# Later attention loads, borrowed buffers for two Fourier evictions, and a rearranged start in a hybrid encoder layer

## The chip, the cores and the metric

The kernel runs on one core of a Trainium2 chip. The core has a matrix engine (TensorE, PE in the profile; its weight loads run beside it as PEld), a vector engine (DVE), a scalar engine (ACT), GpSimd (POOL), and a sync engine (SP) that here only issues DMAs. Each engine works through its own queue in order; they wait for each other by semaphores. The metric is the device time of one execution in microseconds (us), as the median of several runs.

## The reference

One layer of an encoder is applied to two batches of 2048 rows of 1024 features, with the same weights. Rows are normalised, projected into six blocks of columns (q, k, v, the attention gate ga, the Fourier input f and its gate gf), and go through two branches:

```
u = rmsnorm(h, g_norm)
q, k, v, ga, f, gf = split(u @ w_in)
q, k = rope(rmsnorm(q, g_q)), rope(rmsnorm(k, g_k))
a  = attention(q, k, v) * silu(ga)                   # 8 q heads, 2 kv heads, width 64
fo = real(fft2(f over rows, channels)) @ w_fmix * silu(gf)
h  = h + concat(a, fo) @ w_out
h  = h + (p @ w_ple) * sigmoid(rmsnorm(h, g_ple) @ w_ple_gate)
y  = rmsnorm(h, g_final)
```

All is in float32. The kernel makes float32 products on TensorE from float16 pairs (a high part and a residual, three products each).

## The kernel before

There are two parts. **project()** runs over 16 chunks of two tiles of 128 rows (eight chunks for each batch). For a chunk it loads the rows x, squares them on ACT (sq_u), takes a reciprocal root on DVE (newton), writes the high part on ACT (hi_u) and the residual on DVE, and has SP transpose both by DMA into uc (lo_u). PE multiplies uc with the weights of kv and q (mm_tile), and in a sweep with those of f, gf and ga (sweep_f, sweep_ga). ACT evicts, DVE and POOL do norms and rope, and SP stores q, k and v transposed to DRAM (qTd, kTd, vd); POOL's queue stores gates and the first Fourier stage (gd). The second part interleaves **attention()** (64 units of eight steps; a unit is a batch, a kv head and 128 queries) with the second Fourier stage (**fourier2()**), then with the output projection.

The order of everything in project() is written out by hand: within an engine the instructions stand as the code calls them. What the change touches:

- **The weights** (weights(), line 293). A block of w_in comes in eight pieces of 128 rows. For each block DVE scans all eight for the largest magnitude (L312), POOL reduces that over partitions, DVE makes a scale from it (L272 to L328), and then for each piece ACT writes the high part (L334) and DVE the residual (L335). Only then can PE use it. It is a generator: a `next` takes one step (a load, a scan, a split), and `until(g, "loaded")` or `until(g, "split")` runs it to that point. There are generators for kv, q, ga, and one in rest() for f, gf and what is wanted later.
- **The places of the pieces** (places()). In the early phase, pieces are loaded into buffers of the pool A1 that other tiles will use later: names such as qn, t2, z, t1. f's and gf's pieces take a ring of ten 2-KB buffers (w2k, shown as w_st).
- **The written-out start** (lines 839 to 900), before the loop `for i in range(2, n + 4): iteration(i)`. It interleaves the first chunks (0 to 4 of the 16) with the weights. The maxima of v (VL, the vmax instructions) release the kv products' banks in PSUM.
- **early()** (L1682), called at iteration n - 3. It closes the pool of x and the high/residual tiles and opens the pool kv in its place; attention() up to its first `yield` then issues on SP the loads of k and v of both kv heads and of q for units 0, 1 and 2; fourier_first() opens the pool F0 and loads the tables and rows for the first two Fourier tiles (c2, c2x, g_in).
- **leads()** runs the row maxima (a_mx, L1193) of attention's first units inside project()'s last iterations. They use PSUM banks of the pool ps_x that the sweeps use too.
- **fourier2()** evicts the first products of each tile t into fT (L1079), a tile of the pool B, which takes memory that project()'s tiles had. mix() then multiplies fT with bd, which SP loads first of all in fourier2().
- **The exponentials' buffers** are seven tiles p32 of the pool att, each [128, 2, 512] in float32 (L1149).

SP's queue is where loads, transposes and stores of project() stand in one line. A store of v (vd) frees the tile vs, which ACT writes again two chunks later (L679).

Of the kernel before, what the change touches and what calls it, by code (L numbers as in the profile page):

```python
# [10 lines left out]
F32 = mybir.dt.float32  # L11
# [25 lines left out]
FP = 2  # L37
# [3 lines left out]
P32 = 7  # L41
# [99 lines left out]
class Build:  # L141
# [421 lines left out]
        v = self.a["x_prompt" if s == 0 else "x_sample"]  # L563
        return v.rearrange("o (t r) d -> t (o r) d", t=NT)[t]

    def project(self, P, PU, W, early, wkv, wq, wga, bg, mid):

# [215 lines left out]
        def iteration(i):  # L785
            nonlocal stores, stores_next
            if ok(i + 4):
                load_x(i + 4, 0)
            if ok(i - 1):
                load_rope(i - 1)  # L790
            stores, stores_next = stores_next, []
            for f in stores:
                f()
            del stores[:]
            if ok(i + 3):
                sq_u(i + 3)
            sq = square_z(i - 1) if ok(i - 1) else None
            if ok(i - 1) and i > 2:
                VL.pop((i - 1, 1))()
            if ok(i - 3):  # L800
                lo_q(i - 3)
            if ok(i - 2):
                rope_q(i - 2)
            rs = None
            if ok(i - 1) or ok(i + 2):
                rs = newton(i - 1 if ok(i - 1) else None, i + 2 if ok(i + 2) else None, sq)
            if ok(i):
                mm_tile(i, 0)
            if ok(i):
                sweep_part(4.0)  # L810
                VL.pop((i, 0))()
            sweep_part(1000.0 if i < n else (6.0, 9.0, 5.0, 100.0)[i - n])
            if ok(i - 1):
                norm_q(i - 1, rs)
            if ok(i + 2):
                hi_u(i + 2)
                for tt in range(CH):
                    lo_u(i + 2, tt)
            if ok(i + 4):
                load_x(i + 4, 1)  # L820
            if ok(i - 2):
                hi_q(i - 2)
            if ok(i):
                mm_tile(i, 1)
                append(i)
            if i == n - 3:
                early()
            if i == n + 3:
                self.drain(bg)
                self.drain(self.ahead)  # L830
                self.last_stores = nc.gpsimd
                for f in stores_next:
                    f()
                del stores_next[:]

        both = lambda f, i: [f(i, tt) for tt in range(CH)]
        both(load_x, 0)
        until(wkv, "loaded")  # L840
        both(load_x, 1)
        sq_u(0)
        newton(None, 0, None)
        hi_u(0)
        for _ in range(3):
            next(wkv)
        both(lo_u, 0)
        until(wq, "loaded")
        until(wkv, "split")
        both(mm_kv, 0)  # L850
        until(bg, "loaded")
        sq_u(1)
        for _ in range(4):
            next(wq)
        newton(None, 1, None)
        hi_u(1)
        for _ in range(5):
            next(wq)
        lo_u(1, 0)
        next(wq)  # L860
        lo_u(1, 1)
        until(wq, "split")
        both(mm_q, 0)
        both(load_x, 2)
        load_rope(0)
        for _ in range(4):
            next(wga)
        both(mm_tile, 0)
        VL.pop((0, 0))()
        both(mm_kv, 1)  # L870
        both(mm_q, 1)
        until(bg, "split")
        until(wga, "loaded")
        load_x(3, 0)
        both(mm_tile, 1)
        for x in ((0, 1), (1, 0), (1, 1)):
            VL.pop(x)()
        for f in stores_next:
            f()
        del stores_next[:]  # L880
        append(0)
        until(bg, "split")
        sweep_part(10.4)
        sq_u(2)
        newton(None, 2, None)
        hi_u(2)
        both(lo_u, 2)
        load_x(3, 1)
        both(load_x, 4)
        until(bg, "split")  # L890
        next(bg)
        sweep_part(11.6)
        mid()
        sq_u(3)
        make_u(3, 0)
        both(load_x, 5)
        sq_u(4)
        sweep_part(1000.0)
        append(1)
# [83 lines left out]
    def fourier2(self, pool, hook):  # L983
# [82 lines left out]
        for t in range(16):  # L1066
# [2 lines left out]
                yield "half"  # L1069
            loads(t + FP)  # L1070
            g, c = [G.pop((t, i)) for i in range(2)], C.pop(t)
            fT = pool.tile([128, 4, 2, 128], F32, name="fT", bufs=2)
            fx = None
            for i in range(2):
                ps = self.bank()
# [40 lines left out]
    def attention(self, kvp):  # L1116
# [136 lines left out]
        for kv in range(2):  # L1253
            load_kv(0, kv)
            load_q(kv)
        load_q(2)
        nm = kvp.tile([128, 4, 128], F16, name="nm", bufs=1)
        nc.gpsimd.memset(nm[:], 0.0)
        kone = kvp.tile([128, 128], F16, name="kone", bufs=1)
# [15 lines left out]
                    max_rows(0)  # L1275

        self.ahead = leads()
        pool = yield 0.0
        self.ones = pool.tile([128, 64], F32, name="ones", bufs=1)
        nc.gpsimd.memset(self.ones[:], 1.0)  # L1280
        fresh = {last[0, kv]: kv for kv in range(2)}
# [389 lines left out]
    def run(self):  # L1671
# [5 lines left out]
        with pool("psA", 5, space=PSUM) as self.psX, pool("A", side="right") as A:  # L1677
            with pool("A1", side="right") as A1:
# [3 lines left out]
                def early():  # L1682
                    u_stack.close()
                    KV = w_stack.enter_context(pool("kv"))
                    self.atts = self.attention(KV)
                    next(self.atts)
                    self.fourier_first(w_stack.enter_context(pool("F0")))

                W, self.WF = {}, {}
# [7 lines left out]
                WP = w_stack.enter_context(pool("wts", 3))  # L1697
                held = {}

                def places(tags, m):  # L1700

                    def stage(k, cols):
                        if k % m == 0:
                            tag, n = tags[k // m]
                            held[tag, k // m] = A1.tile([128, m, cols], F32, name="w_" + tag, tag=tag, bufs=n)
                        t = held[tags[k // m][0], k // m]
                        if k % m == m - 1:
                            del held[tags[k // m][0], k // m]
                        return t[:, k % m, :]
                    return stage  # L1710

                def stage(k, cols):
# [5 lines left out]
                        return self.WF[n]  # L1718
                    return go

                wkv = self.weights([block("kv", lambda: W["kv"])], places([("qn", 1), ("t2", 1)], 4), 8)
                wq = self.weights([block("q", lambda: W["q"])], places([("z", 2), ("z", 2), ("t1", 2), ("t1", 2)], 2), 8)

                def mid():
                    self.setup2(A1)
                    self.scales()
                    self.scale_a()

                wga = self.weights([block("ga", wtile("ga"))], places([("qn", 1), ("t2", 1), ("t1", 2), ("t1", 2)], 2), 8)

                def rest():
                    wf = self.weights([block(n, wtile(n)) for n in ("f", "gf")], stage, 8)
                    for g, scale in ((wf, self.scale_f), (wf, self.scale_gf), (wga, self.scale_ga)):
                        for x in g:
                            if x == "split":
                                scale()
                            yield x
                            if x == "split":
                                break
                    yield True  # L1740
                    for n in range(2):
                        c = slice(n * 512, (n + 1) * 512)
                        yield from self.weight_far(f"wo{n}", a["w_out"][0][:, c], 512, None, A1)
# [3 lines left out]
                    yield from self.channel_map(A1)  # L1747
                    self.scales3()

                self.project(A1, AU, W, early, wkv, wq, wga, rest(), mid)  # L1750
                manual.__exit__(None, None, None)
        self.psX = None
        att_stack = ExitStack()
        WP1 = w_stack.enter_context(pool("wts1"))
        AP = att_stack.enter_context(pool("att"))
        self.psS = att_stack.enter_context(pool("psS", 2, space=PSUM))
        self.psM = att_stack.enter_context(pool("psM", 1, space=PSUM))
        self.psO = att_stack.enter_context(pool("psO", 1, space=PSUM))
# [104 lines left out]
```

## Time and profile before

| | |
|---|---|
| median of 3 runs | 2685.51 us (2683.37 to 2689.4) |
| profiled execution | 2686.84 us, span 2685.1 us |
| PE busy | 2615.4 us, 97% |
| DVE, ACT, POOL busy | 1612.6, 1186.0, 1634.4 us |
| mean granted PE clock | 0.992 |
| moved by DMA | 305.37 MB, mean 114 GB/s |

The profile is of one execution. Rows of the timeline give start, duration, engine, line and operation, output and inputs, and in brackets the idle time just before with what ended it; SPq is SP issuing a DMA (no busy time). Rows of stages give the busy time of PE, PEld, DVE, ACT and POOL with counts in brackets, then the clock granted to PE, the share of DMA engines busy and GB/s. Rows of waits give who waited for whom, in total, how often, and the longest. Rows of DMA issues give the size of one and the median time from issue to landing.

### The profile page before, as it was taken

The page shows a single profiled execution, that of the slowest core. Times are in us where ns is not written, and L with a number is a line of the kernel's source. Part 1 is how long each engine was busy: PE and PEld are TensorE (multiplying, and loading weights), DVE is VectorE, ACT ScalarE, POOL GpSimd, SP SyncE. Part 2 cuts the span into 40 slices and gives each one's busy share as a digit, 9 for nine tenths or more (in the row PEclk, how much of TensorE's full clock was granted, in tenths as well). Part 3 has the DMA queues.
Part 4 walks back from the last instruction along what each step waited for, and adds up shares of the span by engine and source line. Part 5 has one row for each costly group of instructions (what it writes and reads, how often), then busy time and mean ns, then how long its engine had stood idle before and what let it go on. Part 6 is the DMA issues. An engine that isn't in the chain of part 4 may idle for free. (4 is left out here: it accounts for less than half of the span.)

```text
span 2685.1 us, 49976 instructions
## 1 busy us (share of the span) xinstructions
PE 2615.4 (97%) x20096; PEld 1401.6 (52%) x20096; DVE 1612.6 (60%) x2300; ACT 1186.0 (44%) x1983; POOL 1634.4 (61%) x1376
## 2 busy tenths in 40 slices
PE   5899999999999999999999999999999999999998
PEld 3465565655556664545455554444454544555443
DVE  6756565565446675666675656655565666656634
ACT  4543333333224553554444545445444444444442
POOL 1233232242236886787787777777777877777760
PEclk9999999999999999999999999999999999999999
DMA  8467576685617774222322223332232322232222
GB/s 238 133 178 200 175 195 188 165 196 145 172 56 207 238 214 111 55 62 74 80 68 66 60 68 91 97 74 67 69 87 62 74 77 76 63 83 75 64 76 73
DMA packets 453385, 305.37 MB, mean 114 GB/s; under 512 B 294272, under 2 KB 394816, under 8 KB 453152
## 3 DMA queue, kind: packets, MB, share of 16 engines
q1 hardware_dynamic: 440240, 260.41, 37.9%
q0 software_dynamic: 12912, 41.77, 4.2%
q8 instruction: 157, 2.57, 0.4%
q14 instruction: 76, 0.62, 0.1%
HBM read 149.50 MB, written 86.51 MB: 88 GB/s over the span
## 5 line engine op out<-in xcount | busy, mean ns | idle before, releaser
L1166 POOL TENSOR_TENSOR acc<-acc,p 128x1024 f32<-128x1024 f32 x384 | 919.9, 2396 | 195.7 <-ACT p L1161 159.6
L1193 DVE TENSOR_REDUCE a_mx<-ps_m 128x1 f32<-128x1024 f32 x498 | 609.3, 1223 | 564.1 <-PE ps_m L1185 555.2
L1161 ACT ACTIVATE p<-ps_s,s_scale 128x512 f32<-128x512 f32 x1024 | 648.1, 684 | 653.6 <-PE ps_s L1158 647.0
L1472 PE MATMUL ps_g<-w_pg,hT 64*128 64x512 f16 x2784 | 493.1, 376 | 1.5 <-DVE h L1398 0.8
L451 PEld LDWEIGHTS <-uc 128*128 128x128 f16 x3072 | 301.9, 98 | 320.8 <-issue 33.0
L1221 PE MATMUL ps_o<-p,v 128*64 128x256 f32 x4096 | 467.7, 381 | 0.0
L1158 PE MATMUL ps_s<-q,k 64*128 64x512 f16 x3072 | 433.7, 378 | 5.1 <-ACT p L1161 4.9
L1221 PEld LDWEIGHTS ps_o<-p,v 128*64 128x64 f32 x4096 | 288.6, 137 | 166.0 <-issue 27.7
L1472 PEld LDWEIGHTS <-hT 64*128 64x128 f16 x2784 | 205.2, 94 | 155.7 <-issue 13.5
L1472 PE MATMUL ps_g<-w_wo,mh 64*128 64x512 f16 x1440 | 259.8, 377 | 1.2 <-DVE seen L1438 1.2
L1472 PE MATMUL ps_g<-w_wo,mT 64*128 64x512 f16 x1440 | 256.2, 376 | 0.0
L1158 PEld LDWEIGHTS <-k 64*128 64x128 f16 x3072 | 151.1, 94 | 200.0 <-issue 76.9
L1185 PE MATMUL ps_m<-k,q 64*128 64x512 f16 x996 | 200.0, 377 | 4.5 <-DVE a_mx L1193 4.3
L1164 POOL TENSOR_TENSOR acc<-p,p 128x1024 f32<-128x1024 f32 x64 | 150.9, 2358 | 69.3 <-ACT p L1161 68.7
L451 PEld LDWEIGHTS <-w_ga 128*128 128x128 f16 x1536 | 149.2, 98 | 39.3 <-issue 11.1
L935 POOL DMA_DIRECT2D gfd<-gt x32 | 19.7, 616 | 234.3 <-DVE gt L963 201.0
L1472 PEld LDWEIGHTS <-mh 64*128 64x128 f16 x1440 | 100.1, 94 | 90.8 <-issue 18.0
L1472 PEld LDWEIGHTS <-mT 64*128 64x128 f16 x1440 | 102.7, 94 | 81.3 <-issue 3.8
L1243 DVE RECIPROCAL ps_f<-ps_f 128x256 f32<-128x256 f32 x63 | 110.7, 1756 | 21.2 <-PE ps_f L1236 21.2
L451 PE MATMUL ps_x<-w_f,uc 128*128 128x512 f16 x480 | 105.9, 379 | 0.0
L451 PE MATMUL ps_x<-uc,w_ga 128*128 128x256 f16 x936 | 105.5, 273 | 0.0
L1228 ACT ACTIVATE at<-ps_o,a_scale 128x256 f32<-128x256 f32 x64 | 30.3, 474 | 165.9 <-PE ps_o L1221 165.9
(319 smaller groups left out, 3188.5 us busy)
## 6 DMA issues: line engine op xcount, KB each, us to landing
q<-qTd SPq DMA_DIRECT2D x256, 64.0 KB, 2.3
ag<-agd SPq DMA_DIRECT2D x64, 256.0 KB, 3.3
out<-h POOLq DMA_DIRECT2D x31, 512.0 KB, 3.0
x<-in_x_prompt SPq DMA_DIRECT2D x16, 512.0 KB, 5.0
gfd<-gt POOLq DMA_DIRECT2D x32, 256.0 KB, 2.7
gd<-ge POOLq DMA_DIRECT2D x32, 256.0 KB, 2.9
agd<-gat POOLq DMA_DIRECT2D x64, 128.0 KB, 3.0
w_st<-in_w_out SPq DMA_DIRECT2D x32, 256.0 KB, 3.8
```

What stands on the lines that cost most here:

```text
L451: self.nc.tensor.matmul(ps, lhs(ia, k), rhs(ib, k), start=(i == 0), stop=(i == 3 * ks - 1))
L935: lambda t=t, gt=gt: nc.gpsimd.dma_start(self.gfd[s][t], gt[:]))
L1158: nc.tensor.matmul(S[u][e][:], w[sl], q[sl].rearrange("p h q -> p (h q)"), start=j == i == 0, stop=i + 1 == len(todo), skip_group_check=True)
L1161: nc.scalar.activation(p[:, e, :], S[u][e][:], AF.Exp, scale=self.sc["s_scale"][:])
L1164: nc.gpsimd.tensor_tensor(out=ACC[u][:], in0=P[u, 0][:], in1=p[:], op=ALU.add)
L1166: nc.gpsimd.tensor_tensor(out=ACC[u][:], in0=ACC[u][:], in1=p[:], op=ALU.add)
L1185: nc.tensor.matmul(ps[c], Q[u][0][sl, h, :], kt[s, kv, half][sl, :, 0, :], start=True, stop=True)
L1193: nc.vector.reduce_max(MX[u][:, h, half, c:c + 1], x, axis=AX.X)
L1221: nc.tensor.matmul(o[64 * f:64 * f + 64], vt[s, kv, c // 8][:, c % 8, :], p[:, e, f], start=(c == 0), stop=(c == 15))
L1228: nc.scalar.activation(at[:].rearrange("p c q -> p (c q)"), o, AF.Copy, scale=self.sc["a_scale"][:])
L1243: nc.vector.reciprocal(r, r)
L1472: nc.tensor.matmul(g[0][:], g[1](ia, k)[sl], g[2](ib, k)[sl], start=a, stop=z, skip_group_check=True)
```

## The change

It has three parts.

**Late loads.** early() still loads k and v of both heads and q of units 0 and 1. A new function later(), called at iteration n, three iterations on, loads q of unit 2 and runs fourier_first().

**Fourier evictions.** fT of the first two Fourier tiles is taken from the exponentials' buffers, p32 of the pool att, instead of the pool B.

**The start.** q's first five pieces are loaded ahead of the first transposes, the rest right behind them, and x of chunk 1 after that. q's scans come before the reciprocal root of chunk 1, and q's whole split before chunk 1's high parts and residuals. f, gf and ga have a generator each; gf's pieces go into buffers of uc, qs and qT. ga's and gf's pieces are loaded together after f's split; x of chunk 3 and half of chunk 4 are loaded right behind those pieces, and chunk 2 is normalised before gf's split instead of after it. places() takes the number of pieces for each buffer.

```
-    def project(self, P, PU, W, early, wkv, wq, wga, bg, mid):
+    def project(self, P, PU, W, early, later, wkv, wq, wf, wgf, wga, bg, mid):
...
             if i == n - 3:
                 early()
+            if i == n:
+                later()
...
+        def some(g, k):
+            for _ in range(k):
+                next(g)
+
         both(load_x, 0)
         until(wkv, "loaded")
-        both(load_x, 1)
+        some(wq, 5)
         sq_u(0)
         newton(None, 0, None)
         hi_u(0)
-        for _ in range(3):
-            next(wkv)
+        some(wkv, 3)
         both(lo_u, 0)
         until(wq, "loaded")
+        both(load_x, 1)
         until(wkv, "split")
         both(mm_kv, 0)
-        until(bg, "loaded")
+        until(wf, "loaded")
         sq_u(1)
-        for _ in range(4):
-            next(wq)
+        some(wq, 9)
         newton(None, 1, None)
+        until(wq, "split")
         hi_u(1)
-        for _ in range(5):
-            next(wq)
-        lo_u(1, 0)
-        next(wq)
-        lo_u(1, 1)
-        until(wq, "split")
+        both(lo_u, 1)
         both(mm_q, 0)
+        some(wf, 9)
         both(load_x, 2)
+        until(wga, "loaded")
+        until(wgf, "loaded")
+        both(load_x, 3)
+        load_x(4, 0)
         load_rope(0)
-        for _ in range(4):
-            next(wga)
         both(mm_tile, 0)
-        VL.pop((0, 0))()
+        until(wf, "split")
+        self.scale_f()
         both(mm_kv, 1)
         both(mm_q, 1)
-        until(bg, "split")
-        until(wga, "loaded")
-        load_x(3, 0)
+        VL.pop((0, 0))()
+        VL.pop((0, 1))()
+        sq_u(2)
+        some(wgf, 9)
+        newton(None, 2, None)
         both(mm_tile, 1)
-        for x in ((0, 1), (1, 0), (1, 1)):
-            VL.pop(x)()
+        hi_u(2)
+        until(wgf, "split")
+        self.scale_gf()
+        both(lo_u, 2)
+        load_x(4, 1)
+        load_x(5, 0)
+        for tt in range(CH):
+            VL.pop((1, tt))()
+        some(wga, 9)
+        append(0)
+        sweep_part(10.4)
+        until(wga, "split")
+        self.scale_ga()
...
-            fT = pool.tile([128, 4, 2, 128], F32, name="fT", bufs=2)
+            fT = (pool.tile([128, 4, 2, 128], F32, name="fT", bufs=2) if t >= FP else
+                  self.att.tile([128, 4, 2, 128], F32, name="fT", tag="p32", bufs=P32))
...
-        load_q(2)
...
         self.ahead = leads()
-        pool = yield 0.0
+        yield
+        load_q(2)
+        pool = yield
...
+                def later():
+                    next(self.atts)
                     self.fourier_first(w_stack.enter_context(pool("F0")))
...
+                wgf = self.weights([block("gf", wtile("gf"))],
+                                   places([("uc", 3, 4), ("qs", 1, 2)] + [("qT", 2, 1)] * 2), 8)
```

PE's instructions and their order are the same in both kernels, and so are POOL's. Three places of the order matter below.

SP's queue at the start of the program, before (x are rows, uc the transposed rows; w_qn and w_t_116 hold kv's pieces, w_z and the next two w_t q's, w_st f's):

```order
L595 DMA x<-in_x_prompt 128x1024 x2
L304 DMA w_qn<-in_w_in 128x256 x4
L304 DMA w_t_116<-in_w_in 128x256 x4
L595 DMA x<-in_x_prompt 128x1024 x2
L444 DMA_TRANSPOSE uc<-hl 128x16x128 x2
L304 DMA w_z<-in_w_in 128x512 x4
L304 DMA w_t_173<-in_w_in 128x512 x2
L304 DMA w_t_176<-in_w_in 128x512 x2
L304 DMA w_st<-in_w_in 128x512 x8
L444 DMA_TRANSPOSE uc<-hl 128x16x128 x2
```

The same place in the changed kernel, from kv's pieces on to ga's and gf's (w_uc, w_qs, w_qT are gf's):

```order
L304 DMA w_t_116<-in_w_in 128x256 x4
L304 DMA w_z<-in_w_in 128x512 x4
L304 DMA w_t_127<-in_w_in 128x512
L444 DMA_TRANSPOSE uc<-hl 128x16x128 x2
L304 DMA w_t_127<-in_w_in 128x512
L304 DMA w_t_172<-in_w_in 128x512 x2
L595 DMA x<-in_x_prompt 128x1024 x2
L304 DMA w_st<-in_w_in 128x512 x8
L444 DMA_TRANSPOSE uc<-hl 128x16x128 x2
L595 DMA x<-in_x_prompt 128x1024 x2
L304 DMA w_qn<-in_w_in 128x512 x2
L304 DMA w_t_431<-in_w_in 128x512 x2
```

Five of q's pieces moved ahead of the first transposes, and x of the second chunk moved from ahead of them to behind all of q's. Behind the last row shown, four more of ga's pieces, eight of gf's and three x tiles follow before the next transposes.

DVE at q's factor, a piece of the difference (w_mx are scans, w_m the scale's maximum, n_ms the start of the reciprocal root of chunk 1):

```order
 L335 SCALAR_TENSOR_TENSOR wr_kv<-w_t_116,w_gs,wr_kv 128x256 x4
 L312 TENSOR_REDUCE w_mx<-w_z 128x1 x4
+L312 TENSOR_REDUCE w_mx<-w_t_127 128x1 x2
+L312 TENSOR_REDUCE w_mx<-w_t_172 128x1 x2
+L317 TENSOR_TENSOR w_m_295<-w_mx,gn 128x8
+L320 TENSOR_REDUCE w_m_297<-w_m_295 128x1
 L619 MEMSET n_ms 128x20
 L621 TENSOR_SCALAR n_ms<-n_su 128x2
```

The last four scans stood behind the reciprocal root and now stand ahead of it; the scale's remaining steps stay behind it.

SP's queue behind early()'s loads for the first two units, before (q are the third unit's queries, c, c2x and g_in the Fourier loads, vd a store of v):

```order
L1144 DMA q_0_7187<-qTd 64x512 x2
L1144 DMA q_0_7188<-qTd 64x512 x2
L975 DMA c_0_7201<-in_c_dft 128x256
L979 DMA g_in_7203<-gd 128x512
L979 DMA g_in_7205<-gd 128x512
L981 DMA c2x<-in_c_dft2x 128x128
L975 DMA c_1_7208<-in_c_dft 128x256
L979 DMA g_in_7210<-gd 128x512
L979 DMA g_in_7212<-gd 128x512
L584 DMA rt<-in_c_rope 128x2x128
L684 DMA vd<-vs 128x2x64
```

In the changed kernel rt and vd stand right behind the second unit's queries, and the eleven loads stand here, three iterations on, between the transpose of mr (the first unit's row maxima) and project()'s last stores:

```order
L1217 DMA_TRANSPOSE mr<-nm 128x4x128
L1152 DMA q_0_8269<-qTd 64x512 x2
L1152 DMA q_0_8270<-qTd 64x512 x2
L982 DMA c_0_8279<-in_c_dft 128x256
L986 DMA g_in_8281<-gd 128x512
L986 DMA g_in_8283<-gd 128x512
L988 DMA c2x<-in_c_dft2x 128x128
L982 DMA c_1_8286<-in_c_dft 128x256
L986 DMA g_in_8288<-gd 128x512
L986 DMA g_in_8290<-gd 128x512
L684 DMA vd<-vs 128x2x64
L746 DMA qTd<-qT 128x1024 x2
```

The eleven moved past the stores and transposes of three iterations.

More of the change, by code (lines that the diff above doesn't have):

```diff
@@ L880, in project @@
         del stores_next[:]
[L881 to L891, printed above, removed]
+        sq_u(3)
         sweep_part(11.6)
         mid()
-        sq_u(3)
         make_u(3, 0)
-        both(load_x, 5)
+        load_x(5, 1)
         sq_u(4)
@@ L1698, in run, with places @@
                 held = {}
-                def places(tags, m):
+                def places(tags):
+                    slots = [(tag, n, m, j, i) for i, (tag, n, m) in enumerate(tags) for j in range(m)]
                     def stage(k, cols):
[L1703 to L1709, printed above, removed]
+                        tag, n, m, j, i = slots[k]
+                        if j == 0:
+                            held[tag, i] = A1.tile([128, m, cols], F32, name="w_" + tag, tag=tag, bufs=n)
+                        t = held[tag, i]
+                        if j == m - 1:
+                            del held[tag, i]
+                        return t[:, j, :]
                     return stage
@@ L1719, in wtile @@
                     return go
-                wkv = self.weights([block("kv", lambda: W["kv"])], places([("qn", 1), ("t2", 1)], 4), 8)
-                wq = self.weights([block("q", lambda: W["q"])], places([("z", 2), ("z", 2), ("t1", 2), ("t1", 2)], 2), 8)
+                wkv = self.weights([block("kv", lambda: W["kv"])], places([("qn", 1, 4), ("t2", 1, 4)]), 8)
+                wq = self.weights([block("q", lambda: W["q"])], places([("z", 2, 2)] * 2 + [("t1", 2, 2)] * 2), 8)
+                wf = self.weights([block("f", wtile("f"))], stage, 8)
                 def mid():
@@ L1727, in mid @@
                     self.scale_a()
-                wga = self.weights([block("ga", wtile("ga"))], places([("qn", 1), ("t2", 1), ("t1", 2), ("t1", 2)], 2), 8)
+                wga = self.weights([block("ga", wtile("ga"))], places([("qn", 1, 2), ("t2", 1, 2)] + [("t1", 2, 2)] * 2), 8)
+                wgf = self.weights([block("gf", wtile("gf"))],
+                                   places([("uc", 3, 4), ("qs", 1, 2)] + [("qT", 2, 1)] * 2), 8)
                 def rest():
[L1732 to L1740, printed above, removed]
                     for n in range(2):
@@ L1748, in rest @@
                     self.scales3()
-                self.project(A1, AU, W, early, wkv, wq, wga, rest(), mid)
+                self.project(A1, AU, W, early, later, wkv, wq, wf, wgf, wga, rest(), mid)
                 manual.__exit__(None, None, None)
@@ L1754, in run @@
         WP1 = w_stack.enter_context(pool("wts1"))
-        AP = att_stack.enter_context(pool("att"))
+        self.att = AP = att_stack.enter_context(pool("att"))
         self.psS = att_stack.enter_context(pool("psS", 2, space=PSUM))
```

## The prediction

> **What bounds the kernel now.** I read the head of the page first, then a table by stage, then who TensorE (PE) waited for. Times are us; the clock column (PEclk) is the granted share of PE's full rate.
>
> ```profile
> span 2685.1 us, 49976 instructions
> ```
> ```profile
> PE 2615.4 (97%) x20096; PEld 1401.6 (52%) x20096; DVE 1612.6 (60%) x2300; ACT 1186.0 (44%) x1983; POOL 1634.4 (61%) x1376
> ```
> ```profile
> 17.90:105.70 87.80, 70.74 (x388) 39.23 (x389) 65.77 (x181) 41.41 (x73) 4.71 (x8) 0.90 0.59 177
> 105.70:690.00 584.30, 584.30 (x3508) 347.50 (x3507) 338.72 (x763) 216.38 (x384) 204.28 (x195) 1.00 0.67 178
> 690.00:740.00 50.00, 43.67 (x235) 22.67 (x234) 22.65 (x55) 7.43 (x14) 11.11 (x14) 0.93 0.67 193
> 836.00:860.00 24.00, 20.29 (x146) 14.21 (x145) 8.43 (x10) 10.93 (x19) 9.92 (x7) 0.86 0.96 280
> 860.00:2685.10 1825.10, 1800.74 (x15250) 922.17 (x15246) 1113.05 (x1136) 879.05 (x1439) 1357.77 (x1100) 1.00 0.33 86
> ```
> ```profile
> PE ps_x L451 <- DMA uc<-hl: 17.9, 1, 17.9
> PE ps_x L451 <- ACT wr_q L334: 8.7, 1, 8.7
> PE ps_f L451 <- ACT w_ga L334: 7.3, 1, 7.3
> PE ps_x L451 <- DVE a_mx L1193: 6.3, 1, 6.3
> PE ps_f L1077 <- ACT fT L1079: 3.0, 1, 3.0
> ```
> PE is the bound: 2615 of 2685 are busy, and from 105.7 to 690 it never pauses. What can be won lies in a few holes. Behind the first 17.9 (rows, norm, first transposes) stand four: 8.7 for q's split weights, 7.3 for ga's, 6.3 for a maximum on DVE, 3.0 for an eviction on ACT. The change keeps every PE instruction and their order, and aims at these four. Time taken from a hole is kept to the end, if no later one opens, since everything after is laid out by one order and PE-bound.
>
> A hole costs more than its length, because the clock drops behind it:
> ```profile
> 715.00:721.80 6.80, 6.03 (x16) 2.16 (x16) 2.51 (x5) 0.95 (x2) 0.00 (x0) 0.55 0.82 175
> 844.70:851.50 6.80, 6.49 (x31) 4.88 (x32) 1.23 (x1) 4.42 (x8) 3.92 (x2) 0.54 0.80 238
> ```
> 6.03 busy at 0.55 is 3.3 of work: 2.7 lost. 6.49 at 0.54 loses 3.0.
>
> **The change, term A: the start (up to PE's first ga products).** For q I follow DVE and DMA.
> ```profile
> w_t<-in_w_in SPq DMA_DIRECT2D x2, 256.0 KB, 5.6
> ```
> ```profile
> 25.42 0.14 DVE L621 TENSOR_SCALAR n_ms<-n_su 128x2 f32<-128x2 f32 x1
> 27.98 2.19 ACT L640 ACTIVATE hl<-x,rsq_z 128x1024 f16<-128x1024 f32 x2 [5.69 <-DVE rsq_z L258]
> 32.99 2.56 ACT L334 ACTIVATE wr_q<-w_z,w_gs 128x512 f16<-128x512 f32 x4 [2.82 <-DVE w_gs L328]
> 36.71 2.73 DVE L335 SCALAR_TENSOR_TENSOR wr_q<-w_t,w_gs,wr_q 128x512 f16<-128x512 f32 x4
> 92.33 0.61 PE L451 MATMUL ps_f<-uc,w_ga 128*128 128x256 f16 x2 [7.34 <-ACT w_ga L334]
> 97.88 8.02 PE L451 MATMUL ps_x<-uc,w_ga 128*128 128x256 f16 x72
> 40.00:45.00 5.00, 5.00 (x25) 2.25 (x23) 2.22 (x5) 0.94 (x3) 0.00 (x0) 1.00 1.04 382
> ```
> Five of q's eight loads now stand ahead of the first transposes, so their scans need no wait. But the factor's arithmetic still stands behind the reciprocal root (rsqrt) of chunk 1's rows on DVE, and those rows' loads are now behind all of q's. Before, q's last load (issued near 21.9, landing 5.6 later) was down at 27.5. Three q loads (0.75 MB) and two x tiles (1 MB) take its place, seven eighths of the 2 MB: 26.8 at 0.65 for 256 KB (382 GB/s), and 0.4 for the first transposes, which stand behind 1.3 MB where 1 MB stood: 27.2. A square takes about 1.2, the rsqrt 2.5 (25.42 to 27.95), the factor 0.8: ACT starts q's split at 31.7, not 32.99. Its last residual ends near 37.9 (0.8 behind ACT, two runs of 2.73) where it ended at 39.4. The hole shrinks by only 1.3, and the clock still drops in it.
>
> From there the chain of DVE and ACT decides. Durations:
> ```profile
> 42.99 4.83 DVE L312 TENSOR_REDUCE w_mx<-w_st 128x1 f32<-128x512 f32 x8
> 49.60 5.01 ACT L334 ACTIVATE w_f<-w_st,w_gs 128x512 f16<-128x512 f32 x8 [1.68 <-DVE w_gs L328]
> 50.36 5.39 DVE L335 SCALAR_TENSOR_TENSOR w_f<-w_st,w_gs,w_f 128x512 f16<-128x512 f32 x8 [0.79 <-ACT w_f L334]
> 82.55 2.48 DVE L649 SCALAR_TENSOR_TENSOR hl<-x,rsq_z,hl 128x1024 f16<-128x1024 f32 x2 [1.22 <-ACT hl L640]
> ```
> A block is a scan of 4.8, 1.8 to the first ACT split (47.8 to 49.6), 6.15 to the last residual (55.75). So: chunk 1's residuals end at 40.4; f's scan 45.2, its split 47.0 to 53.2; small work to 54.0. gf's scan waits for loads: behind the second transpose (queue free near 43.6) come 1 MB of x, 2 MB for ga, 2 MB for gf. The first piece lands some 2.8 later (an estimate: half of the 5.6 above, where others stood ahead); with 20 pieces of 256 KB at 0.65 the last is down at about 59.4. Scan ends 60.0, rsqrt of chunk 2 by 62.9, its high parts on ACT (2.2) to 65.1, gf's split 65.1 to 71.3. Its residuals and small work run to 74.7, ga's scan to 79.5, its split 81.3 to 87.5. PE ends its first ga group at 87.9; before it went on from there at 97.88. **A = 10.0.** PE by itself would reach ga at about 84 (92.33 less 7.34 is 85.0 before, less the 1 won at q), so DVE, not PE, is late there, by some 1.2. Bounds: 12 if the chain runs clear (PE's own arrival and 2.6 for the group), 6.5 if x or gf's loads are 3.5 later. Hidden work: f's and gf's chain lies beside PE's 46 to 84 with 5 to spare (gf wanted at 72, first piece at 66.6); the v maxima moved behind chunk 2's residuals (74.7) free a bank wanted at 78 (72 and one gf tile). Each us past that cover costs a us.
>
> **Term B: early(), 690 to 722.**
> ```profile
> 700.83 4.92 SPq L1144 DMA_DIRECT2D q<-qTd  x8
> 709.84 0.47 SPq L684 DMA_DIRECT2D vd<-vs  x1
> 714.51 0.28 ACT L679 ACTIVATE vs<-ps_g 128x128 f32<-128x128 f32 x1 [15.98 <-DMA vd<-vs]
> 715.03 2.47 DVE L1193 TENSOR_REDUCE a_mx<-ps_x 128x1 f32<-128x512 f32 x4
> 715.77 8.00 PE L451 MATMUL ps_x<-w_gf,uc 128*128 128x512 f16 x24 [6.33 <-DVE a_mx L1193]
> ```
> The waits table names a_mx, but the cause is SP: ACT cannot write vs until a store of vd lands, that store stands behind 31 loads in SP's queue, and DVE's maximum stands behind it. Eleven of the 31 (q of the third unit, the Fourier tables and rows) go. q's other four end near 703.3, rt takes 0.45, so the store goes out at 703.8, 6.0 sooner. At the same 4.7 to vs and 1.26 from vs to PE, PE is released at 709.75; it wanted 709.44. Left: 0.3 of 6.3, and with no hole the 2.7 of slow clock go. **B = 8.7.** Bounds: 9 if the store lands sooner, 5 if it takes 3 longer behind k and v, since the clock would then drop again.
>
> **Term C: the Fourier start.**
> ```profile
> 837.88 1.16 PE L1077 MATMUL ps_f<-c,g_in 128*128 128x128 f32 x8
> 843.19 0.37 SPq L750 DMA_DIRECT2D kTd<-kT  x1
> 843.80 0.32 SPq L1060 DMA_DIRECT2D bd<-bdd  x1
> 844.27 0.69 ACT L1079 ACTIVATE fT<-ps_f,h_gf 128x512 f32<-128x512 f32 x1 [5.26 <-DMA qTd<-qT]
> 845.01 2.08 PE L1077 MATMUL ps_f<-c,g_in 128*128 128x128 f32 x8 [3.02 <-ACT fT L1079]
> 848.27 0.64 PE L1185 MATMUL ps_m<-k,q 64*128 64x512 f16 x2
> 848.84 0.80 PE L1034 MATMUL ps_g<-bd,fT 128*128 128x128 f32 x2
> ```
> ```profile
> bd<-bdd SPq DMA_DIRECT2D x1, 512.0 KB, 3.5
> ```
> fT's eviction waited for stores out of buffers that its memory held before. In an exponentials' buffer it needs PE alone, so PE runs on at 842.0 instead of 845.0. But what is late next stands close: PE then has 1.1, a score step and a maximum, about 2.5, and at 844.5 wants bd, which SP issues at 843.80 (behind the last kTd store) and which lands 3.5 later, at 847.3. The hole moves from 842 to 844.5 and is 2.8 long; PE reaches L1034 1.5 sooner. If the clock drops again for 6.8, that costs 3.0, against the 1.2 that before still had to lose behind 848.84: **C = 1.5 + 1.2 - 3.0 = -0.3**; without a drop +2.7. I take the drop, since a hole of 3.02 brought it before. Bounds -3.5 (SP's tail 1.7 later behind the eleven loads, and the drop) and +4.
>
> [...]
>
> **Sum.** 10.0 + 8.7 - 0.3 = 18.4 off the profiled execution's 2686.84 (its span and 1.7 around it) is 2668.4. The median of the runs shown, 2685.51, is 1.3 lower; I forecast 2667.
>
> **The rivals.** (1) No drop behind bd, or DVE's chain at the start clear: 2 to 6 better, 2661 to 2665. For it: the hole behind bd is shorter than any that dropped the clock for 6.8 here. [...] Chance 0.22. (2) New waits take a good part: x of chunk 1 or gf's loads land 3.5 later (A 6.5), or the vd store lands 3 later (B 5): 3.5 to 9 worse, 2670.5 to 2676. For it: up to 5 MB queue without a gap at the start, and transposes run between them. Chance 0.20. (3) The change does not do what it says: the holes only move, as the third does in my forecast; if A gives only the 1 of the q hole and B nothing, 2685. Against it: no other late wait is visible in either row set. Chance 0.04. (4) Slower: the eleven late loads. They now go out behind the transpose of mr:
> ```profile
> 810.09 1.89 SPq L1209 DMA_TRANSPOSE mr<-nm  x1
> ```
> from 812 on, about 0.5 each, and land by some 822; PE wants g_in at 837.9, so 16 are spare. Past that each us is a us of PE, plus 3 for the clock. To turn 18.4 into a loss they must land after 853, four times as long as eight q loads took. Chance 0.03.
>
> **How the numbers follow.** Forecast 0.51 (2665 to 2670.5), rivals as above. About 0.2% (5.4 us) is what a measurement of this kernel can tell from no change. Eight in ten: from 2660.5, a little past (1), to 2676, the end of (2). Faster 0.93 (the forecast, (1) and (2)), same 0.04, slower 0.03.
>
> **What would show it.** Right: PE's wait for w_ga gone or spread over 1 to 2 with DVE's w_ga residuals as releaser, first ga group done near 88; the wait for wr_q 7 to 8, still there; vs released near 708 and no PE wait over 1 at 709; at the Fourier start the wait for fT gone and one of 2 to 3 for bd, with a clock row near 0.55. Wrong: a PE wait for uc before chunk 1's kv products; a PE wait for g_in or q; gf's scan waiting on DMA past 61; PE held at L1077 or by exponentials for want of a buffer.

## The result and the profile after

The changed kernel takes 2670.55 us (median of six, 2667.9 to 2672.3) against 2686.29 before (median of six): a ratio of 0.9941 with a 95% interval of 0.993 to 0.9953, 15.7 us. The forecast was 2667.0, 18.4 us by its sum. The profiled execution took 2671.73, its span is 2670.0.

The head of the page after, and PE's waits over 1 us at the start, at early() and at the Fourier start (who waits, for whom; us in total, times, longest):

```profile
span 2670.0 us, 49974 instructions
```
```profile
PE 2611.3 (98%) x20096; PEld 1400.3 (52%) x20096; DVE 1612.9 (60%) x2300; ACT 1184.7 (44%) x1983; POOL 1630.1 (61%) x1376
```
```profile
PE ps_x L451 <- ACT wr_kv L334: 17.5, 1, 17.5
PE ps_x L451 <- ACT wr_q L334: 7.1, 1, 7.1
PE ps_g L1041 <- DMA bd<-bdd: 4.8, 1, 4.8
PE ps_f L451 <- DVE w_ga L335: 1.4, 7, 0.4
PE ps_f L451 <- ACT w_ga L334: 1.3, 1, 1.3
```

Of the four holes the one for a_mx is gone, the 7.3 for w_ga has become 2.7 in eight pieces, the one for wr_q is 1.6 shorter. In place of the 3.0 for fT there is one of 4.8 for bd.

Where did the time come from? The table takes the moment at which PE starts the same instruction in four executions, from the timeline: before, after, and the changed kernel twice more (below). The last column but one is the forecast of what each stretch gains, the last what it gained in the three executions of the changed kernel.

| up to (on PE) | before | after | again | third | forecast | gain |
|---|---|---|---|---|---|---|
| ga's first group done | 97.88 | 89.96 | 90.57 | 90.53 | A 10.0 | 7.9, 7.3, 7.4 |
| second gf tile behind early() | 724.99 | 707.91 | 708.52 | 708.48 | B 8.7 | 9.2, 9.2, 9.2 |
| first Fourier product with c | 837.88 | 819.65 | 820.27 | 820.22 | 0 | 1.2, 1.1, 1.2 |
| first products of p and v | 856.60 | 839.42 | 839.84 | 838.99 | C -0.3 | -1.1, -0.9, -0.1 |
| the same, twelve such groups on | 1028.91 | 1012.98 | 1011.26 | 1011.86 | 0 | -1.3, 0.9, -0.6 |
| end of span | 2685.1 | 2670.0 | 2667.2 | 2669.2 | 0 | -0.8, 0.3, -1.2 |

The sums are 15.1, 17.9 and 15.9. The first two rows carry nearly everything. The last two rows together are -2.1, 1.2 and -1.8: what comes behind 860 differs by 3 us between executions of one and the same kernel.

**The start.** The timeline of after (start, us, engine, line, operation, out<-in; in brackets the idle time before it and its releaser):

```profile
31.73 2.56 ACT L334 ACTIVATE wr_q<-w_z,w_gs 128x512 f16<-128x512 f32 x4 [3.32 <-DVE w_gs L328]
45.05 1.05 SPq L595 DMA_DIRECT2D x<-in_x_prompt  x2
51.01 2.93 SPq L304 DMA_DIRECT2D w_uc<-in_w_in  x4
57.59 2.69 DVE L312 TENSOR_REDUCE w_mx<-w_uc 128x1 f32<-128x512 f32 x4 [4.17 <-DMA w_uc<-in_w_in]
84.42 0.39 PE L451 MATMUL ps_f<-uc,w_ga 128*128 128x256 f16 x2 [1.25 <-ACT w_ga L334]
89.96 8.02 PE L451 MATMUL ps_x<-uc,w_ga 128*128 128x256 f16 x72
```

In this execution q's split starts at 31.73, as forecast (31.7); in the two others it starts at 33.33 and 33.35. SP has its queue free for loads only at 45.05 (forecast 43.6), ga's eight loads stand first, gf's first piece goes out at 51.01, and DVE's scan of it waits 4.17. From there the chain of DVE and ACT is late, PE is paced piece by piece through ga's first group, and ends it at 89.96 instead of 87.9.

**early().** The same view, and the table by stage (from:to, us, then busy time and count of PE, PEld, DVE, ACT and POOL, granted clock, DMA share, GB/s):

```profile
696.17 0.38 SPq L684 DMA_DIRECT2D vd<-vs  x1
699.52 0.28 ACT L679 ACTIVATE vs<-ps_g 128x128 f32<-128x128 f32 x1 [8.91 <-DMA vd<-vs]
701.35 5.34 PE L451 MATMUL ps_x<-w_gf,uc 128*128 128x512 f16 x24
```
```profile
690.00:740.00 50.00, 50.00 (x294) 27.57 (x293) 24.54 (x64) 10.63 (x20) 14.99 (x17) 1.00 0.45 131
```

The store of vd goes out 13.67 sooner than before (709.84), 7.9 of it the start's. It lands in 3.35 instead of 4.67 (131 GB/s move in this stretch, 193 before); PE never pauses and the clock, 0.93 here before, stays at 1.00. The 9.2 are the 6.3 of the hole and 2.9 of slow clock.

**The Fourier start.**

```profile
804.46 1.22 DVE L741 TENSOR_TENSOR qs<-t,qs 128x1024 f16<-128x1024 f32 x1
806.71 2.63 SPq L745 DMA_TRANSPOSE qT<-qs  x2
...
818.72 3.29 SPq L748 DMA_TRANSPOSE kT<-ks  x1
820.85 0.69 ACT L1087 ACTIVATE fT<-ps_f,h_gf 128x512 f32<-128x512 f32 x1
826.69 0.32 SPq L1067 DMA_DIRECT2D bd<-bdd  x1
830.47 0.79 PE L1041 MATMUL ps_g<-bd,fT 128*128 128x128 f32 x2 [4.85 <-DMA bd<-bdd]
```
```profile
828.00:832.00 4.00, 1.53 (x7) 1.53 (x8) 0.00 (x0) 0.51 (x1) 2.34 (x1) 0.52 0.98 285
832.00:836.00 4.00, 4.00 (x25) 3.64 (x26) 0.00 (x0) 0.99 (x2) 0.00 (x0) 0.62 0.84 240
```

The products of fT wait no more, PE runs on to those with bd, and bd is not there. The clock drops (0.52 and 0.62 above), as it did behind fT (0.54).

### The profile page after: what moved, and what is told of

Same layout as the page of the kernel before. It is cut to its first block, busy times and chain, and to the rows that moved or that the text cites. A ratio compares the mean times of both kernels' runs of the same rounds, so it can differ in the third digit from the quotient of the medians.

```text
span 2670.0 us, 49974 instructions
## 1 busy us (share of the span) xinstructions
PE 2611.3 (98%) x20096; PEld 1400.3 (52%) x20096; DVE 1612.9 (60%) x2300; ACT 1184.7 (44%) x1983; POOL 1630.1 (61%) x1376
## 4 chain that ended last, share of the span: by engine, by line
PE 49%; DVE 2%; ACT 1%; issue 0%; DMA 0%; DVEq 0%; SPq 0%; ACTq 0%
PE ps_g L1481 19%; PE ps_o L1229 12%; PE ps_s L1166 10%; PE ps_m L1193 3%; PE ps_f L451 3%; PE ps_x L451 2%; PE ps_f L1244 1%; DVE h L1521 0%; DVE a_mx L1201 0%; PE ps_g L451 0%; ACT p L1169 0%; DVE h_hl L1535 0%; ACT sq L1502 0%; DVE ps_f L1429 0%; ACT h_hl L1502 0%
## 5 line engine op out<-in xcount | busy, mean ns | idle before, releaser
L451 PEld LDWEIGHTS <-w_ga 128*128 128x128 f16 x1536 | 148.8, 98 | 33.6 <-issue 11.1
L1481 PEld LDWEIGHTS <-mh 64*128 64x128 f16 x1440 | 99.8, 94 | 91.2 <-issue 18.4
```

Of the source, the lines that this page charges most:

```text
L451: self.nc.tensor.matmul(ps, lhs(ia, k), rhs(ib, k), start=(i == 0), stop=(i == 3 * ks - 1))
L1481: nc.tensor.matmul(g[0][:], g[1](ia, k)[sl], g[2](ib, k)[sl], start=a, stop=z, skip_group_check=True)
```

## The experiments

The runs are told by chip, each with the median that before had on that chip.

### The three parts alone (before here: 2687.28)

1. Before with the late loads alone:

```diff
+            if i == n:
+                later()
...
-                    self.fourier_first(w_stack.enter_context(pool("F0")))
+                def later():
+                    next(self.atts)
+                    self.fourier_first(w_stack.enter_context(pool("F0")))
...
```

> The kernel before with the late loads alone (q of the third unit and the Fourier tables and rows move three iterations later). Theory (term B stands alone): PE's 6.3 wait for a_mx near 709 goes, the half clock behind it too, and the time falls by 8.5 to 9.5 us, to about 2677. Rival (the eleven loads come out behind SP's tail and push the stores and bd at the Fourier start later): the hole there grows by 2 to 3 us and the gain is only 5 to 7, about 2680.

Measured: 2678.29, ratio 0.9968 (0.9956 to 0.9981), 9.0 us less. The waits of PE:

```profile
PE ps_x L451 <- ACT wr_q L334: 6.9, 1, 6.9
PE ps_m L1187 <- DVE a_mx L1195: 4.8, 9, 1.3
PE ps_f L1079 <- ACT fT L1081: 4.3, 1, 4.3
```

The 6.3 for a_mx is gone (what is left is nine short ones in the attention, 1.3 at most), and from ga's first group (97.42) to the second gf tile (715.38) PE takes 617.96, as after (617.95), where before took 627.11: B alone is 9.15. The hole for fT has grown from 3.0 to 4.3, the rival's mechanism, at half its size.

2. The start's new order alone: the changed kernel with early() and fT's pool put back.

> The changed kernel with the late loads and fT's buffers put back as before, so the start's new order alone. Theory (term A as the changed kernel's trace shows it, 7.9): 2678.4, with gf's scan still waiting about 4 us for its loads at 57 us. Rival 1 (the full 10.0 of the forecast): 2676. Rival 2 (the start's gain is partly given back where the loads of 700 us and the stores meet): 2681 or more.

Measured: 2676.15, ratio 0.9956 (0.9943 to 0.9968), 11.1 us less. PE ends ga's first group at 89.51, 8.4 sooner. In six other executions with this start and ga's loads first it is 6.3 to 8.5 sooner; they differ in the first wait, for the first rows (17.2 to 19.1). The time is nearer to rival 1, but the trace is not: 8.4 is there at 90 us, and 1.2 more comes where neither theory had anything, at early(). There the hole for a_mx is still 6.4 long, but the two gf tiles behind it take 7.96 from start to start instead of 9.22 before (the first alone 6.74 for 8.00, and 5.34 where the clock stays at 1.00): by this, less of the half clock fell on them in this execution. Another 0.9 comes up to the first Fourier product (827.49 against 837.88) and 0.6 behind it, where holes of 2.1 for fT and 1.2 for bd are left and the clock does not drop (behind the first, its products with bd take 0.39 each, as in run 12 at 1.00; in after they take 0.63).

3. Before with fT of the first two rows in the exponentials' buffers.

```diff
-            fT = pool.tile([128, 4, 2, 128], F32, name="fT", bufs=2)
+            fT = (pool.tile([128, 4, 2, 128], F32, name="fT", bufs=2) if t >= FP else
+                  self.att.tile([128, 4, 2, 128], F32, name="fT", tag="p32", bufs=P32))
```

> The kernel before with fT of the first two rows in the exponentials' buffers, nothing else. Theory (the hole only moves from fT to bd): PE's 3.0 wait for fT goes, a wait of 2.5 to 5 for bd appears some 3 us later, the half clock stays behind it; the time is within 1.5 us of before (2685 to 2688). Rival (fT's wait was a loss by itself): 3 to 6 us faster, 2680 to 2683, and no PE wait for bd over 1.

Measured: 2686.8, ratio 0.9995 (0.9986 to 1.0004): no difference. Wait and clock:

```profile
PE ps_g L1034 <- DMA bd<-bdd: 2.8, 1, 2.8
```
```profile
844.00:848.00 4.00, 1.54 (x9) 1.54 (x10) 0.91 (x1) 1.53 (x3) 2.52 (x2) 0.87 0.96 284
848.00:852.00 4.00, 4.00 (x26) 3.22 (x25) 0.00 (x0) 1.47 (x3) 0.02 (x1) 0.70 0.83 271
```

The hole moves from fT to bd and is 2.8 long, to the tenth what term C worked out. The clock drops behind it, for 3.4 us: (4 x 0.13 + 4 x 0.30) / 0.5, with the 0.50 that before has in each us from 716 to 721. Before it was 6.8 here. In this execution PE is at the first products of p and v 1.7 sooner (854.88 against 856.60); the medians neither show that gain nor exclude it.

### What makes bd late (before: 2687.28 for the first, 2688.24 for the others)

4. The changed kernel with bd loaded by POOL's queue, so that it does not stand behind the last k store in SP's.

```diff
-        nc.sync.dma_start(self.bd[:], self.bdd)
+        nc.gpsimd.dma_start(self.bd[:], self.bdd)
```

> The changed kernel with the load of bd issued by POOL instead of SP, so that it no longer stands behind the last k store in SP's queue. Theory (bd's place in SP's queue is the whole of what is left at the Fourier start): bd is issued near 822 instead of 826.7, PE's 4.8 wait for it falls below 1, the half clock of 6.8 us behind it goes, and the time falls by 6 to 8 us below the changed kernel, to 2663 to 2665. Rival 1 (without the hole the clock still drops): 4 to 5 us, about 2666. Rival 2 (the next late thing, the rows of gf or POOL's own queue, takes the hole's place): under 2 us, 2669 or more.

Measured: 2671.34, ratio 0.9938 (0.9926 to 0.9951): nothing gained, rival 2. The timeline:

```profile
825.32 0.55 POOL L1067 DMA_DIRECT2D bd<-bdd  x1 [3.60 <-ACT p L1169]
830.03 0.49 PE L1041 MATMUL ps_g<-bd,fT 128*128 128x128 f32 x2 [3.23 <-DMA bd<-bdd]
```
```profile
agd<-gat POOLq DMA_DIRECT2D x4, 128.0 KB, 6.3
```

POOL could not issue it before 825.3. The row names ACT, but ACT's exponentials are no input of a load. In the program it waits for stores of ga's last products, whose memory bd takes; the first of the four went out at 818.75, and they take 6.0 to 6.6 to land. PE's wait for bd is shorter (3.2 for 4.6 to 5.3), but one of 0.95 for g_in follows, and PE is at the products of p and v 18.8 behind its first Fourier product, where the three executions of the changed kernel have 18.8 to 19.8. So SP's queue was not the cause, or not alone.

5. bd and fx in memory that falls free earlier, and bd still on POOL's queue.

```diff
-        nc.sync.dma_start(self.bd[:], self.bdd)
+        first = [w2k("gf_in")]
+        FX = [pool.tile([128, 4, 128], F32, name="fx", bufs=1)]
+        self.bd = pool.tile([128, 2, 4, 128], F32, name="bd", bufs=1)
+        nc.gpsimd.dma_start(self.bd[:], self.bdd)
...
-                self.bd = B.tile([128, 2, 4, 128], F32, name="bd")
```

> The changed kernel with bd and fx in memory that falls free some 10 us earlier (the ropes' and the v pieces' old place instead of the place of ga's last products and of k's halves), and bd issued by POOL, so that neither the last stores of ga's products nor the last k transpose stands before them. Theory (what was left at the Fourier start was memory not yet free, not the queue): bd is issued near 821.6 and lands before PE wants it, fx no longer waits for the transpose, PE's waits for bd and fx fall below 1 in sum, no half clock behind them, and the time falls by 5 to 8 us below the changed kernel. Rival (the next late thing takes the place: the rows g_in of the third table behind the last k store, 1 us before, now 3 to 4, and the clock drops all the same): 0 to 3 us.

Measured: 2675.15, ratio 0.9957 (0.9945 to 0.997), 6.2 above the changed kernel beside it (2668.98). The theory falls, and so does its rival. The DMA view of after, then of this kernel (from issue to landing, in us, last), and a row of this kernel's stages:

```profile
bd<-bdd SPq DMA_DIRECT2D x1, 512.0 KB, 3.7
kT<-ks SPq DMA_TRANSPOSE x1, 7.3
```
```profile
820.29 0.55 POOL L1070 DMA_DIRECT2D bd<-bdd  x1
832.34 0.80 PE L1041 MATMUL ps_g<-bd,fT 128*128 128x128 f32 x2 [7.30 <-DMA bd<-bdd]
```
```profile
bd<-bdd POOLq DMA_DIRECT2D x1, 512.0 KB, 12.0
kT<-ks SPq DMA_TRANSPOSE x1, 13.7
```
```profile
828.00:832.00 4.00, 0.00 (x0) 0.00 (x0) 0.00 (x0) 0.00 (x0) 0.60 (x1) 0.50 0.74 170
```

bd did go out at 820.29, without a wait, so it was the memory that held it in run 4. But it went out beside the transpose of k. Both then took much longer (12.0 for 3.7, 13.7 for 7.3), and the stores of q too (9.9 for 3.7), while the engines moved 170 GB/s where after moved 285 in the same slice; from 820 to 832 it is 169 against 246. In after bd starts behind the transpose and is down at 830.4, 1.9 sooner than in this kernel. POOL's queue was not slow by itself: in run 4, where bd went out 2 us before the transpose was down, it took 4.7. That the meeting, and not bd's other memory, made both slow is the likely reading; the two were not tested apart. By these three kernels, what sets the Fourier start is the last transpose of q and k plus the load behind it; another queue won bd 2 us at most, which the next load took back, and other memory made it later.

### gf's loads first (before: 2688.24)

6. The changed kernel with gf's loads ahead of ga's.

```diff
-        until(wga, "loaded")
         until(wgf, "loaded")
+        until(wga, "loaded")
```

> The changed kernel with gf's eight loads issued ahead of ga's at the start. Theory (the 2.1 us that the start's term fell short are gf's loads, which stand behind ga's 2 MB): gf's scan no longer waits (4.2 us), DVE reaches ga's split some 4 us sooner, PE's first ga group is no longer paced by it and ends near 86 instead of 90, and the time falls by 3 to 4.5 us below the changed kernel. Rival (ga's scan now waits for its loads, or DVE is held by something else, the v maxima or chunk 2's rows): under 1.5 us.

Measured: 2668.1, ratio 0.9926 (0.9913 to 0.9938), 0.9 below the changed kernel beside it. The timeline:

```profile
53.93 2.46 DVE L312 TENSOR_REDUCE w_mx<-w_uc 128x1 f32<-128x512 f32 x4
83.94 2.85 PE L451 MATMUL ps_f<-uc,w_ga 128*128 128x256 f16 x24
86.64 5.62 PE L451 MATMUL ps_x<-uc,w_ga 128*128 128x256 f16 x50
```

At the start all is as expected: the scan does not wait, PE does ga's first group in one run and ends it at 86.64, 3.3 before after and 3.9 before the run beside it. So the order of these loads is what A fell short by; with gf first A is 11.2, and 10.0 to 11.9 in the three other executions with that order (runs 7, 10 and 12). 2.8 of the 3.9 are still there at 1012 us (1008.48 against 1011.26), and 1.6 in the span. In the medians 0.9 is left, which these intervals cannot tell from nothing or from 3.

7. Both of the last two edits together.

> Both edits together. If they are independent, as the theories of both say, the gain below the changed kernel is the sum of the two runs beside it; a rival (what is kept at the start is lost at the Fourier start, as transfers meet differently) gives 2 us less than that sum.

Measured: 2673.27, ratio 0.9947 (0.9934 to 0.9959): 1.9 below run 5, where run 6 had given 0.9. They add up within the noise, and run 5's loss is seen a second time.

8. The changed kernel again, as the measure of the three.

> The changed kernel itself on this chip, so that the three others are compared with it in one place: 15 to 17 us faster than before, near 2670.5.

Measured: 2668.98, ratio 0.9931 (0.9917 to 0.9944): 19.3 less, 2 more than expected; its trace is the column "again" above.

### What the slow clock costs (before: 2687.09, for the last 2686.59)

9. The changed kernel with idle products in the hole, to keep PE busy; they write what the real ones then overwrite.

```diff
                 ps = self.bank()
+                for _ in range(32 if t == 0 and y else 0):
+                    nc.tensor.matmul(ps[:, :128], fT[:, 0, 1, :], fT[:, 0, 0, :], start=True, stop=True)
```

> The changed kernel with 32 products of fT with itself ahead of the first products with bd, into the same bank, where the real products overwrite them: 4.3 us of PE work (8 of that shape take 1.06) laid into PE's wait for bd of 4.8 to 5.3. They compute nothing that is used. Theory (behind that hole the half clock costs 3 us by itself): the wait left is under 1 us, the row of granted clock behind it stays near 1.0, PE reaches the second table's products 2.5 to 3.5 us sooner, and the time falls by as much below the changed kernel. Rival (the transfers, not PE, set the end of that stretch, so that the slow clock is hidden): the clock stays up and the time is the same within 1.

Measured: 2675.58 (one of six times was 12302, the other five have a median of 2674.1), ratio 0.9955 (0.9943 to 0.9967): slower than the changed kernel beside it (2670.94), against both theories.

```profile
827.19 7.41 PE L1039 MATMUL ps_g<-fT 128*128 128x128 f32 x64
```
```profile
832.00:836.00 4.00, 4.00 (x38) 4.00 (x37) 0.00 (x0) 0.00 (x0) 0.83 (x1) 1.00 0.93 270
...
944.00:960.00 16.00, 12.95 (x93) 8.14 (x94) 10.84 (x14) 6.02 (x11) 12.52 (x8) 0.89 0.78 237
```

My estimate was wrong: each of these products in f32 ran as two instructions, so the 32 took 7.41, and PE came to bd at 834.44, 1.9 after it was down (issued at 828.51, 4.0 to landing). The clock did stay at 1.00, and from the first product with bd to the first of p and v PE took 6.70 instead of 8.24 to 8.95 in the three executions of the changed kernel: the slow clock there costs 1.5 to 2.3. Saving and late arrival cancel: PE is at the products of p and v 19.85 behind its first Fourier product, where the three have 18.77 to 19.77. From there to the end of the span it lost 3.9 to 7.1 more than they did, part of it in the second row, a half clock around 955 where the changed kernel had none; the rest was not traced.

10. The same with gf's loads first.

> The same with gf's loads ahead of ga's as well. Theory (gf's loads ahead are worth 3 to 4 us at PE's first ga group and keep at least 2.5 of them to the end): 2 to 4 us below the kernel with the 32 products alone, and 5 to 7 below the changed kernel. Rival (as the single run with gf first measured, 0.9): under 1.5 below the kernel with the 32 products alone.

Measured: 2671.64, ratio 0.9945 (0.9932 to 0.9957): 2.4 to 3.9 below run 9 (by its two medians), as expected, but 0.7 above the changed kernel. Again a slow stretch near 950 follows (clock 0.78 from 948 to 952, 0.80 from 952 to 956).

11. The changed kernel a third time.

> The changed kernel once more beside these two, as their measure: 15 to 19 us faster than before, 2669 to 2671.

Measured: 2670.94, ratio 0.9941 (0.9929 to 0.9953), as expected; its trace is the column "third" above.

12. gf's loads first and 20 idle products.

> gf's loads first and only 20 idle products ahead of bd's: 32 took 7.41 us (each runs as two instructions), so 20 take 4.6, less than the wait of 4.8 to 5.3. Theory (the slow clock behind that hole is worth 1.6 to 2.7, and 32 products gave it back by reaching 2 us past bd's landing): PE reaches bd no later than it lands, the clock stays up there, and the time is 1.5 to 3 below the kernel with gf's loads first alone (2668.1), so about 2666. Rival (what is won there meets the wait for the gathered rows and a later slow window near 945 to 955, as with 32 products): 2667.5 to 2670.

Measured: 2668.93, ratio 0.9935 (0.9921 to 0.9949): the rival. Two stretches:

```profile
816.00:836.00 20.00, 19.06 (x162) 15.19 (x162) 7.56 (x9) 10.54 (x18) 10.02 (x7) 1.00 0.95 285
944.00:956.00 12.00, 9.47 (x65) 5.46 (x65) 7.12 (x8) 5.16 (x10) 11.84 (x8) 0.86 0.70 187
```
```profile
946.33 0.37 PE L1168 MATMUL ps_s<-q,k 64*128 64x512 f16 x1 [2.50 <-ACT p L1171]
```

This time the size is right: no wait for bd and no slow clock at the Fourier start, and PE is at the products of p and v at 834.11, 2.8 before run 6 (836.90). By 963.8 nothing of it is left (963.81 against 963.78). A wait behind the gathered rows (ag, told of in the next section) took it: 2.50 here, 1.36 in run 6, and here the clock drops behind it for 3.4 us, which costs 1.7 more. No version beats the changed kernel by more than these runs can tell: run 6 has the lowest median.

## Why the prediction held, and where it was off

The mechanism was right in its two large steps. The time fell inside the range (2660.5 to 2676), but 0.05 past the end of the forecast's own band (2670.5), where rival (2) begins. That the sum came so near is in part luck: 1.2 that the forecast did not see and 0.5 in B stand against 2.1 to 2.7 missing in A and, in the profiled execution, 0.8 in C. Step by step:

- **A, 10.0: mis-sized.** It measured 7.9 (7.3 and 7.4 in the repeats). The part for q was right only by luck of the profiled execution: split at 31.73, hole 7.1, clock still dropped (0.50 from 33 to 36). In eleven traces with this start the split begins between 31.7 and 34.0, on average at 32.7, against 33.0 in the three with the old one (before, runs 1 and 3): 0.3 sooner, where 1.3 was worked out. The spread passes on: PE ends ga's first group at 89.4 behind a split at 31.72 (run 5) and at 91.6 behind one at 33.95 (run 9). The term that failed is the one for gf's loads: their scan was to end at 60.0 and ended at 62.9. By the forecast's terms gf's first piece, the thirteenth behind the transposes, was to be down at 54.85 (43.6, 2.8 and 13 times 0.65); it came at 57.59. 1.45 of these 2.7 are SP's queue, free at 45.05. About 0.5 is a slip in the working: 256 KB at the 382 GB/s it reads are 0.69, not 0.65, thirteen times over. The rest lies between the queue and the landing; the engines moved 281 GB/s from 45 to 50 and 389 behind that. Run 6 shows that this order of loads is what held A back: with gf's loads first the scan does not wait, and A becomes 11.2 (10.0 to 11.9 in four executions), up to the bound of 12 for a clear chain. Rival (2) named this wait, at 3.5.
- **B, 8.7: right.** 9.2 in all three executions, and 9.15 alone (run 1). Of the half us more, 0.3 is the hole that was to be left: the store landed in 3.35 instead of 4.67, so none was. The rest is the slow clock, 2.9 for 2.7.
- **C, -0.3: the hole right by itself, too short beside the late loads.** Alone (run 3) the hole is 2.8 as worked out, and the time the same. Together with the late loads it is 4.6 to 5.3. One part is what the bound named ("SP's tail 1.7 later behind the eleven loads"), at half its size. PE is 18.2 sooner at the first Fourier product, 17.1 of it from A and B, but the last k transposes only 16.3 (818.72 against 835.05): the tail loses 0.8. It loses it at the transposes of q: their data are written at 805.68, and SP issues them at 806.71; before, they followed in 0.1:

```profile
821.56 1.22 DVE L741 TENSOR_TENSOR qs<-t,qs 128x1024 f16<-128x1024 f32 x1
822.84 2.62 SPq L745 DMA_TRANSPOSE qT<-qs  x2
...
835.05 3.45 SPq L748 DMA_TRANSPOSE kT<-ks  x1
```

  SP issues nothing else between 803.4 and 806.7. Its waits in after have this one:

```profile
SPq L745 <- DMA qTd<-qT: 3.2, 1, 3.2
```

  It waits for the stores of the tile before (qTd), which went out at 801.86 behind the eleven late loads; only when they have landed is qT free to be written again. The wait is in every trace with the late loads (2.6 to 3.9; run 1 alone 3.5) and in none without them (before, runs 2 and 3). Run 1, with late loads and the old fT, has the longer hole too (4.3). The other 1.2 came to PE alone: its wait of 1.1 for ga's last product on DVE fell away. The forecast did not see that gain, and the bd hole took it back at once. Why that wait fell away was not tested; it is gone in run 2 as well, and 0.4 of it is left in run 1.
- **The 6.8 of slow clock, 3.0: too much as a fixed price.** The changed kernel's stretch in the first execution and in the one again:

```profile
820.00:860.00 40.00, 35.09 (x274) 24.55 (x272) 16.97 (x20) 20.40 (x35) 24.71 (x15) 0.91 0.91 260
```
```profile
820.00:860.00 40.00, 34.69 (x276) 24.21 (x274) 17.32 (x22) 20.86 (x34) 25.04 (x17) 0.96 0.91 263
```

  Behind holes of 4.8 and 5.3 that is 7.2 and 3.2 us at half rate (6.9 and 3.4 by rows of 4 us): one kernel, two lengths. Elsewhere too the length does not follow the hole: about 3.4 in runs 4, 1 and 11 (holes of 3.2, 4.3 and 4.6), but 6.8 in before (3.0) and in run 6 (5.3). What sets the length was not tested. The 2.8 of run 3 dropped the clock (0.70 from 848 to 852), and the 2.5 of run 12 too (0.57 from 948 to 952). So the condition of rival (1), no drop behind 2.8, was wrong.
- **Rivals (3) and (4).** The holes of A and B did not move on: from 690 to 740 PE is busy for all of its 50 us, and what A gained is still there. The late loads cost no wait for g_in or q of their own; what they cost is the 0.8 in the tail.

What is behind 860 was no part of the sum and gives or takes up to 2 us. One place can be named, the gathered rows, here in the profiled execution of the changed kernel, with the wait of PE that follows, and in the one again:

```profile
945.41 1.26 POOL L1372 TENSOR_TENSOR ag<-ag 128x512 f32<-128x512 f32 x1 [6.36 <-DMA ag<-agd]
951.46 0.37 PE L1166 MATMUL ps_s<-q,k 64*128 64x512 f16 x1 [2.31 <-ACT p L1169]
```
```profile
944.71 1.27 POOL L1372 TENSOR_TENSOR ag<-ag 128x512 f32<-128x512 f32 x1 [5.26 <-DMA ag<-agd]
```

POOL waits for these loads between 5.1 and 6.7 us. Its products behind them hold ACT and so PE, for 1.1 us (before) to 2.6 (run 9): in all fourteen traces PE's wait is 4.0 to 4.1 shorter than POOL's. Behind 2.3 to 2.6 the clock dropped in runs 9, 10 and 12 (0.57 to 0.82 in rows of 4 us), behind the 2.3 of after not (1.00). What makes these loads quicker or slower was not settled.

## What to carry to other kernels

A load that stands behind others was late here by what the queue issued ahead of it, not by one latency: gf's first piece was down 12.5 us after the queue came free (45.05 to 57.59), where the forecast had allowed 11.25 and q's pieces had taken 5.6 before. So count the loads, and find when the queue itself comes free. When two waits end close together at one place, taking one away, or anything that brings PE there sooner, can lengthen the other (3.0 for fT became 2.8 for bd in run 3, and 4.6 to 5.3 with the other parts), so follow the chain that feeds the second one too; here it runs over the last transposes and moved less than PE (16.3 for 18.2). Loads put later in a queue can delay the stores behind them, and through the buffers that these free the work of the next tile; here SP waited 3.2 for qTd and its tail lost 0.8. Moving a load out of a queue did not help where what it then ran beside was slowed with it (run 5, 13.7 for 7.3).

## What the runs showed of the hardware

- A 512 KB load issued from POOL beside a DMA transpose took 12.0 us, and the transpose 13.7 (run 5), where one after the other they took 3.7 and 7.3 (after); from 820 to 832 us the engines moved 169 GB/s, and 246 one after the other.
- At the Fourier start the half clock lasted about 3.4 us behind holes of 2.8, 3.2, 4.6 and 5.3 (runs 3, 4, 11 and 8), 6.8 to 6.9 behind 3.0, 4.8 and 5.3 (before, after and run 6), and 10.2 behind 7.3 (run 5), by rows of 4 us. Near 950 it came behind waits of 2.3, 2.5 and 2.6 (runs 10, 12 and 9), and not behind the 2.3 of after.
- A product of 128x128 by 128x128 in f32 ran as two instructions: 20 took 4.73 us as 40 (run 12), 32 took 7.41 as 64 (run 9).
